# A hybrid attention and Mamba-2 block on one core: B of groups 1 to 7 is turned into rows through DRAM instead of on TensorE

## The chip, the core and the metric

The kernel runs on one core of a Trainium2 chip. Five engines work side by side, each through its own stream of instructions in a fixed order: TensorE (PE in the profile: matrix products and transposes), VectorE (DVE), ScalarE (ACT), GpSimd (POOL) and SyncE (SP). They wait for each other with semaphores. Transfers run on DMA queues, which SyncE and GpSimd fill here. The metric is the time of one execution on the device in microseconds (us); lower is better.

## What is computed

One layer of a decoder block: 512 tokens, 1024 channels, fp32. Two token mixers take the same normed input: an attention branch (12 heads, three dilated patterns) and an SSM branch (Mamba-2, 8 groups, 4 heads of 64 channels a group, 128 states). Their sum by learned gates goes through an output projection, and then through an MLP of 4096 hidden channels. The change touches the SSM branch alone. From the reference:

```python
xbc = jax.nn.silu(causal_conv(xbc) + conv_b)
xs, bm, cm = jnp.split(xbc, [SSM_INNER, SSM_INNER + SSM_GROUPS * SSM_STATE], axis=-1)
...
# ssd_chunked: 4 chunks c of 128 tokens (l, s), group g, head h of the group, state n, channel p
cb = jnp.einsum('bclgn,bcsgn->bcgls', cc, bc)
y_diag = jnp.einsum('bcghls,bcsghp->bclghp', cb[:, :, :, None] * decay, xd)
states = jnp.einsum('bclgn,bcghl,bclghp->bcghpn', bc, decay_states, xd)
_, prev = lax.scan(step, init, (states, chunk_decay))      # over the chunks
y_off = jnp.einsum('bclgn,bcghpn,bcghl->bclghp', cc, prev, jnp.exp(a_cs))
...
y = (y_diag + y_off + d_skip * xs) * silu(z)
y = rmsnorm_per_group(y, norm_w) @ w_ssm_proj
```

B (bc here) is used twice: in cb with the states as the summed axis, and in the states with the tokens as the summed axis. A product on TensorE sums over the partitions, so B is needed both ways: states on the partitions (as conv leaves it) and tokens on the partitions ("rows").

## The kernel before

**Precision.** A large fp32 product is made as three products of rounded halves: `split` makes the high half on ScalarE (line 96) and the low half as the rest on VectorE (line 99), and `three` issues high x high, high x low, low x high. Names ending in h and l are such halves (xsh, bkl, yth, ytl, wh_x). The scan's products of pcb, pyd, pyo and pn are made in full fp32.

**The weights.** A unit is a block of 256 weight columns, or rows for the projection: x (the SSM input), bc (B and C), z, sp (the SSM projection), gs and ga (gates). `prep` loads a unit through SyncE and splits it into one of two slots of wh and wl. A unit is 48 matmuls of 512 columns. A unit of x, bc or z makes two outputs of 24 matmuls each; sp makes eight outputs of 6. The splits of x's weights are put off (`held`) to the end of the third step of `ssm_group`.

**The order on TensorE.** Every matmul and transpose stays in program order (`mm`, `tr`: lines 227 and 230), and the program is interleaved by hand. `ssm_group(g)` is a generator with a `yield` between the steps of one group's scan; the units stand in a queue, `Filler`. The loop over the groups calls `fill.run(us)` ahead of each step, which issues matmuls of the queue worth that many us at 0.64 us for three of them, and the budgets of the seven steps come from a table, `SSM_FILL`, or `SSM_LAST` for group 7. So the unit matmuls cover the time that the other engines need between two steps. The queue's order is x0, bc0, then for each group x, bc, z, and sp of the group before.

**The steps of a group**, with the names that the profile shows:

1. xd (rows of x times dt), xs (times the decay to the chunk's end), split into xsh and xsl.
2. Three transposes pb turn B's first three chunks into rows, and `split` makes bkh (ScalarE) and bkl (VectorE) of them. Four products pcb of C and B; VectorE masks them into cbm (L812), and multiplies the decays w by cbm in four products (L816).
3. Nine matmuls pst of 256 columns make the states from bkh, bkl, xsh and xsl; the third is the first that reads bkl. VectorE chains them into prev (L826 to L830).
4. Sixteen products pyd of xd and w, six products pyo of prev and C; VectorE makes y of them (L845 to L856), through the scratch tile t1.
5. pn sums the squares of y; VectorE, GpSimd (rt, L215) and two transfers on GpSimd's queue (rt_d L873, rg L875) make the norm's factor as a row for every partition. Then `decays(g+1)` reads the next group's w on that queue (L774).
6. Nothing.
7. y is scaled (L882) and split into yth and ytl (ScalarE L96, VectorE L99), which sp of this group reads later.

VectorE adds each output of sp into acc (L729, `acc_evac`), and in group 0 ScalarE copies it instead. The scheduler places these adds early by a priority; it orders the other engines' instructions by priorities and by when their data come, except where `pin` keeps the program's order.

**x through DRAM.** x also needs rows. `to_rows` transposes 32 by 32 blocks on VectorE (L741), writes them to a scratch tensor in DRAM with four transfers of 64 KB on GpSimd's queue (L744), and `x_unit` reads it back as rows, xd, with one transfer of 512 KB (L757) on the same queue. B doesn't go this way before.

Of the kernel before, what the change touches and what calls it, by code (L numbers as in the profile page):

```python
# [11 lines left out]
F32 = mybir.dt.float32  # L12
# [6 lines left out]
P = 128  # L19
T = 512  # L20
NT = 4
# [5 lines left out]
GROUPS = 8  # L27
# [15 lines left out]
BIG = 1e30  # L43

FILL0, FILL1, FILLA, FILLB, FILLC = 3.0, 4.0, 3.0, 2.8, 2.8
SSM_FILL = (6, 4, 4, 3, 9.5, 5, 4.5)
SSM_LAST = (5, 6, 4, 3, 9, 8, 8)

V_ORDER = tuple((d, i) for d in (1, 0, 2) for i in range(NT))
V_STEPS = {(1, 0, 2): (("s", 2),), (1, 0, 5): (("t", 1),), (1, 0, 6): (("n", 2),), (1, 1, 1): (("s", 3),),  # L50
# [33 lines left out]
def hybrid_block(ctx: ExitStack, tc: tile.TileContext, a: dict):  # L84
    nc = tc.nc
    act, dve, pool, pe, sp = nc.scalar, nc.vector, nc.gpsimd, nc.tensor, nc.sync
# [5 lines left out]
    dram = ctx.enter_context(tc.tile_pool(name="dram", bufs=1, space=DRAM))  # L92


    def split(src, hi, lo, eng=None, pinned=False, lo_pinned=False):
        ins = act.activation(hi, src, AF.Copy)  # L96
        if pinned:
            tc.keep_in_program_order(ins)
        ins = (eng or dve).tensor_tensor(lo, src, hi.bitcast(F32), op=ALU.subtract)  # L99
        if lo_pinned:  # L100
            tc.keep_in_program_order(ins)
# [22 lines left out]
    held = []  # L124
# [37 lines left out]
    def v3(t, k):  # L162
        return t.rearrange("p (k n) -> p k n", k=k)
# [59 lines left out]
    def pin(ins):  # L223
        return tc.keep_in_program_order(ins)
# [4 lines left out]
    def tr(dst, src):  # L229
        tc.keep_in_program_order(pe.transpose(dst, src, ident))  # L230
# [27 lines left out]
    def abank(name):  # L258
        return psa.tile([P, T], F32, name=name, tag="a")
# [256 lines left out]
    def in_unit(key, evac):  # L516

        hi, lo = take(key)
        for c in range(2):
            ps = gbank(f"ps{key}_{c}")  # L520
            yield from gemm_part(ps, v3(hi, KD), v3(lo, KD), c, range(KD), KD, uhk, ulk)
            with tc.high_priority(offset=400):
                evac(c, ps)
        done()
# [103 lines left out]
    for key in ATT_UNITS:  # L628
        n, j = key[:-1], int(key[-1])
# [54 lines left out]
    sg = sctx.enter_context(tc.tile_pool(name="ssm", bufs=1, side="right", reuse_waits="tile"))  # L684
# [4 lines left out]
    def conv_silu(ct, ps, tag, bufs):  # L689
        h = sg.tile([P, T], F32, name=f"ch{ct}", tag="ch", bufs=2)  # L690
        act.activation(h, ps, AF.Identity, bias=cb_[:, ct : ct + 1], scale=cw[:, ct, 3:4])
        for d in (1, 2, 3):
            dve.scalar_tensor_tensor(h[:, d:], ps[:, : T - d], cw[:, ct, 3 - d : 4 - d], h[:, d:],
                                     op0=ALU.mult, op1=ALU.add)
        t = sg.tile([P, T], F32, name=f"ct{ct}", tag=tag, bufs=bufs)
        act.activation(t, h, AF.Tanh)
        dve.scalar_tensor_tensor(t, t, 1.0, h, op0=ALU.add, op1=ALU.mult)
        return t
# [32 lines left out]
        return evac  # L731

    convs = {}
    xrows, xds = {}, {}

    def to_rows(src, rows_, c0, tag, name):


        n = src.shape[-1]
        t = sg.tile([P, n], F32, name=f"sqt{name}", tag=tag, bufs=2)  # L740
        dve.transpose(t, src)  # L741
        for r in range(4):
            rs_ = slice(32 * r, 32 * r + 32)
            ins = pool.dma_start(rows_[:, c0 + 32 * r : c0 + 32 * r + 32].rearrange("(m i) j -> i m j", i=32),  # L744
                                 t[rs_, :].rearrange("i (m j) -> i m j", j=32))
            if c0:
                pin(ins)

    def x_unit(g):
        def evac(c, ps):  # L750
            convs[g, c] = conv_silu(2 * g + c, ps, "cx", 4)
            if c == 0:
                xrows[g] = dram.tile([T, UC], F32, name=f"x_d{g}")
            to_rows(convs[g, c], xrows[g], c * P, "sq", f"{g}_{c}")
            if c == 1:
                xds[g] = sg.tile([P, NT * UC], F32, name=f"xd{g}", tag="xd")
                pin(pool.dma_start(v3(xds[g], NT), xrows[g].rearrange("(k p) j -> p k j", p=P)))  # L757

        return in_unit(f"x{g}", evac)

    def bc_unit(g):
        def evac(c, ps):
            convs[g, 2 + c] = conv_silu(16 + 8 * c + g, ps, "cb" if c == 0 else "cc", 2)

        return in_unit(f"bc{g}", evac)

    TC = T - P
# [20 lines left out]
    def ssm_group(g, sz):  # L788
# [7 lines left out]
        dve.tensor_tensor(h64(xs), h64(xd[:, : 3 * UC]), bc64(ds_, g, 0, 3), op=ALU.mult)  # L796
        xsp = [sg.tile([P, 3 * UC], F32R, name=f"xs{n}{g}", tag=f"xs{n}") for n in "hl"]
        split(xs, *xsp)
        yield

        bt, ct = convs.pop((g, 2)), convs.pop((g, 3))
        bk = [sg.tile([P, TC], F32R, name=f"bk{n}{g}", tag=f"bk{n}") for n in "hl"]
        pb = abank(f"pb{g}")
        for c in range(3):
            tr(pb[:, c * P : (c + 1) * P], bt[:, c * P : (c + 1) * P])
        split(pb[:, :TC], *bk)
        pcb = abank(f"pcb{g}")
        for c in range(NT):
            cs = slice(c * P, (c + 1) * P)
# [4 lines left out]
        for c in range(NT):  # L814
            wv = w[:, c * HG : (c + 1) * HG, :]
            dve.tensor_tensor(wv, wv, cbm[:, c, :].unsqueeze(1).broadcast_to([P, HG, P]), op=ALU.mult)  # L816
        yield

        prev = sg.tile([P, 3, UC], F32, name=f"prev{g}", tag="prev")
        pst = [abank(f"pst{g}_{b}") for b in range(2)]  # L820
        for c in range(3):
            pv = pst[c // 2][:, (c % 2) * UC : (c % 2 + 1) * UC]
            bs, us = slice(c * P, (c + 1) * P), slice(c * UC, (c + 1) * UC)
# [19 lines left out]
        for j in range(2):  # L843
# [6 lines left out]
            t1 = sg.tile([P, TC], F32, name=f"t1{g}_{j}", tag="t1", bufs=2)  # L850
# [46 lines left out]
    for g in range(GROUPS):  # L897
        fill.add(f"x{g}", x_unit(g))
        fill.add(f"bc{g}", bc_unit(g))
        if g == 0:  # L900
            for j in (2, 3):
                fill.add(f"ap{j}", att_unit(j))
        else:
            fill.add(f"z{g}", z_unit(g, szs[g]))
            fill.add(f"sp{g-1}", project_unit(g - 1, acc_evac(g - 1)))
# [4 lines left out]
    for g in range(GROUPS):  # L910
        steps = ssm_group(g, szs[g])
        fill.through(f"bc{g}")
        for n, us in enumerate(SSM_LAST if g == GROUPS - 1 else SSM_FILL):
            fill.run(us)
            if n == 3 and g > 0:
                fill.through(f"z{g}")
            next(steps, None)
# [293 lines left out]
    us = {}  # L1211
# [67 lines left out]
    j = last  # L1279
# [106 lines left out]
```

## Time and profile before

| | |
|---|---|
| time, median of 3 runs (lowest to highest) | 1086.37 us (1086.25 to 1086.47) |
| the profiled execution: its own time | 1084.77 us |
| its span, from the first to the last instruction | 1083.0 us |
| mean granted clock of TensorE | 0.999 |
| TensorE busy | 1068.3 us, 99% of the span |
| VectorE busy | 741.4 us, 68% |
| ScalarE busy | 532.9 us, 49% |
| GpSimd busy | 120.1 us, 11% |

In the stage that holds the scan's groups 0 to 7 (250 to 655 us of the span), the windows view gives 400.1 us of TensorE in 405, 342.1 of VectorE and 212.1 of ScalarE. The time of an execution is longer than its span by what lies around the first and the last instruction (1.8 us here). A row of the timeline has the start and the length of an instruction in us, the engine, its line, the operation with its output and its inputs, the shapes, and how many instructions it stands for; a bracket at its end says how long the engine was idle ahead of it, and for whom.

### The profile page before, as it was taken

What the parts mean: (1) busy time and instruction counts of PE and PEld (TensorE: products, weight loads), DVE (VectorE), ACT (ScalarE), POOL (GpSimd) and SP (SyncE); (2) the same over time, 40 slices, a digit from 0 to 9 for tenths busy, and PEclk for the clock granted to TensorE, in tenths of its full rate; (3) what the DMA queues carried; (4) which work ended last, traced back from release to release, by engine and by line L of the source; (5) the groups of instructions that cost most, each with busy time, mean ns of one, the idle gap of its engine ahead of it and who ended that gap; (6) DMA issues with size and microseconds to landing.
All of it is one profiled execution on the core that took longest, in us unless ns stands there. A gap on an engine that the chain in (4) does not pass through costs nothing.

```text
span 1083.0 us, 14771 instructions
## 1 busy us (share of the span) xinstructions
PE 1068.3 (99%) x5895; PEld 908.5 (84%) x5895; DVE 741.4 (68%) x1104; ACT 532.9 (49%) x921; POOL 120.1 (11%) x159
## 2 busy tenths in 40 slices
PE   9999999999999999999999999999999999999997
PEld 8988787778778878888888878889899998888886
DVE  6657666436877889897979795868687785342324
ACT  6356656526375645546273723454466665332222
POOL 2203122002031211202030300010000000000000
PEclk9999999999999999999999999999999999999999
DMA  8232122224453544434454423540233324233202
GB/s 278 86 102 75 61 78 68 93 83 111 152 126 118 127 132 111 141 103 146 132 143 144 127 91 114 204 146 2 78 121 113 118 81 144 107 124 110 82 35 78
DMA packets 90853, 121.44 MB, mean 112 GB/s; under 512 B 5776, under 2 KB 75920, under 8 KB 89760
## 3 DMA queue, kind: packets, MB, share of 16 engines
q1 hardware_dynamic: 85216, 101.01, 29.1%
q0 software_dynamic: 5424, 19.49, 6.7%
q8 instruction: 46, 0.75, 0.3%
q14 instruction: 23, 0.19, 0.1%
q10 hardware_dynamic: 144, 0.00, 0.0%
HBM read 114.11 MB, written 6.37 MB: 111 GB/s over the span
## 4 chain that ended last, share of the span: by engine, by line
PE 89%; DVE 6%; ACT 1%; issue 1%; DMA 1%; POOL 0%; POOLq 0%; DVEq 0%; ACTq 0%
PE psd L227 16%; PE psx L227 8%; PE psbc L227 8%; PE psz L227 8%; PE psuX L227 6%; PE pssp L227 5%; PE psu L227 4%; PE psga L227 4%; PE psgs L227 4%; PE psv L227 3%; PE psk L227 3%; PE psq L227 3%; PE psuZ L227 3%; PE psap L227 3%; PE psuY L227 1%; PE pq L227 1%
## 5 line engine op out<-in xcount | busy, mean ns | idle before, releaser
L227 PE MATMUL psd<-wh_dn,hh 128*128 128x512 f32 x240 | 93.4, 389 | 0.0
L227 PE MATMUL psd<-wl_dn,hh 128*128 128x512 f32 x240 | 93.4, 389 | 0.0
L227 PE MATMUL psd<-wh_dn,hl 128*128 128x512 f32 x240 | 93.4, 389 | 0.0
L99 DVE TENSOR_TENSOR hl<-hidden,hh 128x512 fp32r<-128x512 f32 x31 | 21.1, 692 | 71.4 <-ACT hh L96 71.3
L96 ACT ACTIVATE hh<-hidden 128x512 fp32r<-128x512 f32 x31 | 19.1, 628 | 92.0 <-PE psd L227 92.0
L227 PEld LDWEIGHTS psd<-wh_dn,hl 128*128 128x128 f32 x240 | 45.0, 188 | 9.4
L227 PEld LDWEIGHTS psd<-wh_dn,hh 128*128 128x128 f32 x240 | 45.0, 188 | 9.4
L227 PEld LDWEIGHTS psd<-wl_dn,hh 128*128 128x128 f32 x240 | 45.0, 188 | 9.2
L227 PE MATMUL psx<-uh,wl_x 128*128 128x512 f32 x128 | 50.0, 390 | 1.8 <-DVE wl_x L99 1.8
L227 PE MATMUL pssp<-yth,wh_sp 128*128 128x512 f32 x128 | 51.1, 400 | 0.0
L227 PE MATMUL psx<-uh,wh_x 128*128 128x512 f32 x128 | 50.6, 396 | 0.0
L227 PE MATMUL pssp<-ytl,wh_sp 128*128 128x512 f32 x128 | 50.2, 392 | 0.3 <-DVE ytl L99 0.3
L227 PE MATMUL pssp<-yth,wl_sp 128*128 128x512 f32 x128 | 50.1, 392 | 0.0
L227 PE MATMUL psz<-uh,wh_z 128*128 128x512 f32 x128 | 50.0, 391 | 0.0
L227 PE MATMUL psbc<-uh,wh_bc 128*128 128x512 f32 x128 | 49.9, 390 | 0.0
L227 PE MATMUL psz<-uh,wl_z 128*128 128x512 f32 x128 | 49.9, 390 | 0.0
L227 PE MATMUL psx<-ul,wh_x 128*128 128x512 f32 x128 | 49.8, 389 | 0.0
L227 PE MATMUL psz<-ul,wh_z 128*128 128x512 f32 x128 | 49.8, 389 | 0.0
L227 PE MATMUL psbc<-uh,wl_bc 128*128 128x512 f32 x128 | 49.8, 389 | 0.0
L227 PE MATMUL psbc<-ul,wh_bc 128*128 128x512 f32 x128 | 49.8, 389 | 0.0
L744 POOL DMA_DIRECT2D x_d<-sqt x64 | 41.6, 657 | 72.8 <-DVE sqt L741 72.3
L96 ACT ACTIVATE wh_bc<-ws_bc 128x1024 fp32r<-128x1024 f32 x16 | 16.7, 1055 | 60.6 <-PE pssp L227 53.3
(362 smaller groups left out, 3291.6 us busy)
## 6 DMA issues: line engine op xcount, KB each, us to landing
ws_up<-in_w_up_dram SPq DMA_DIRECT2D x16, 1024.0 KB, 5.6
ws_dn<-in_w_down_dram SPq DMA_DIRECT2D x15, 1024.0 KB, 5.0
ws_z<-in_w_in_dram SPq DMA_DIRECT2D x8, 1024.0 KB, 7.5
ws_x<-in_w_in_dram SPq DMA_DIRECT2D x8, 1024.0 KB, 6.3
w<-acs_d POOLq DMA_DIRECT2D x8, 1024.0 KB, 5.8
ws_bc<-in_w_in_dram SPq DMA_DIRECT2D x16, 512.0 KB, 5.2
ws_sp<-in_w_ssm_proj_dram SPq DMA_DIRECT2D x8, 1024.0 KB, 4.9
ws_ga<-in_w_in_dram SPq DMA_DIRECT2D x4, 1024.0 KB, 6.0
```

What stands on the lines that cost most here:

```text
L96: ins = act.activation(hi, src, AF.Copy)
L99: ins = (eng or dve).tensor_tensor(lo, src, hi.bitcast(F32), op=ALU.subtract)
L227: tc.keep_in_program_order(pe.matmul(*args, **kw))
L744: ins = pool.dma_start(rows_[:, c0 + 32 * r : c0 + 32 * r + 32].rearrange("(m i) j -> i m j", i=32), t[rs_, :].rearrange("i (m j) -> i m j ...
```

## The change

Three things change together. First, the rows of B in groups 1 to 7 no longer come from transposes on TensorE. When conv has made B, its first three chunks go through `to_rows` as x does: a 32 by 32 transpose on VectorE (128 x 384, into a buffer of t1), four writes to b_d on GpSimd's queue, and a read back into br (192 KB, tag t1) on that queue, all pinned to the program's order. Group 0 keeps the transposes. Second, the split into bkh and bkl stands behind the second `yield`, ahead of pst, in those groups. Third, the table of budgets: group 0 gets one of its own, and the budgets ahead of the second and third steps grow while the fifth shrinks, so that more of sp lies ahead of pcb and pst and less ahead of pn. `while held and g == 0` in the first step finds nothing to do in the order that is built. All lines behind the tables move down by one, and by up to eleven in `ssm_group`.

```diff
-SSM_FILL = (6, 4, 4, 3, 9.5, 5, 4.5)
-SSM_LAST = (5, 6, 4, 3, 9, 8, 8)
+SSM_FIRST = (6, 4, 4, 4, 8.5, 5, 4.5)
+SSM_FILL = (6, 6, 4.5, 3.5, 7, 5, 4.5)
+SSM_LAST = (6, 7, 5, 4, 8, 8, 8)
...
     def to_rows(src, rows_, c0, tag, name):
...
-            if c0:
+            if c0 or tag == "t1":
                 pin(ins)
...
     def bc_unit(g):
         def evac(c, ps):
             convs[g, 2 + c] = conv_silu(16 + 8 * c + g, ps, "cb" if c == 0 else "cc", 2)
+            if c == 0 and g > 0:
+                rows_ = dram.tile([TC, P], F32, name=f"b_d{g}")
+                to_rows(convs[g, 2][:, :TC], rows_, 0, "t1", f"b{g}")
+                brs[g] = sg.tile([P, TC], F32, name=f"br{g}", tag="t1", bufs=2)
+                pin(pool.dma_start(v3(brs[g], NT - 1), rows_.rearrange("(k p) j -> p k j", p=P)))
...
         split(xs, *xsp)
+        while held and g == 0:
+            held.pop()()
         yield
...
-        pb = abank(f"pb{g}")
-        for c in range(3):
-            tr(pb[:, c * P : (c + 1) * P], bt[:, c * P : (c + 1) * P])
-        split(pb[:, :TC], *bk)
+        if g == 0:
+            pb = abank(f"pb{g}")
+            for c in range(3):
+                tr(pb[:, c * P : (c + 1) * P], bt[:, c * P : (c + 1) * P])
+            split(pb[:, :TC], *bk)
         pcb = abank(f"pcb{g}")
...
         yield
+        if g > 0:
+            split(brs.pop(g), *bk)
...
-        for n, us in enumerate(SSM_LAST if g == GROUPS - 1 else SSM_FILL):
+        for n, us in enumerate(SSM_FIRST if g == 0 else SSM_LAST if g == GROUPS - 1 else SSM_FILL):
```

On TensorE, groups 2 to 6 have, before: 48 matmuls of z, the 3 of pb, pcb, 18 of sp, the 9 of pst, 15 of sp, pyd and pyo, 15 of sp, 30 of x, pn, 18 of x, 48 of bc. Now: 48 of z, 9 of sp, pcb, 21 of sp, the 9 of pst, 18 of sp, pyd and pyo, 33 of x, pn, 15 of x, 48 of bc. Group 1 goes from z to sp, 12, to pcb, and then has 21 of sp ahead of pst; group 7 has 15 ahead of pcb and 24 between pcb and pst.

The order on VectorE changes at the middle of each group. In group 3 before, from cbm to the first of the four products of w (acc0 and so on are the adds of sp's outputs, pssp2 those of group 2):

```order
L812 TENSOR_TENSOR cbm3_3751<-pcb3_3746,tri_198 128x512
L543 SCALAR_TENSOR_TENSOR sz3_1_3757<-sz3_1_3757,psz3_1_3706 128x512
L99 TENSOR_TENSOR xsl3_3717<-xs3_3714,xsh3_3716 128x768
L729 TENSOR_TENSOR acc0_2897<-acc0_2897,pssp2_0_3762 128x512
L729 TENSOR_TENSOR acc1_2906<-acc1_2906,pssp2_1_3770 128x512
L99 TENSOR_TENSOR bkl3_3739<-pb3_3740,bkh3_3738 128x384
L816 TENSOR_TENSOR w3_3530<-w3_3530,cbm3_3751 128x512
L729 TENSOR_TENSOR acc2_2915<-acc2_2915,pssp2_2_3778 128x512
```

And now, in the same group:

```order
L730 TENSOR_TENSOR acc0_2887<-acc0_2887,pssp2_0_3762 128x512
L100 TENSOR_TENSOR xsl3_3736<-xs3_3733,xsh3_3735 128x768
L821 TENSOR_TENSOR cbm3_3781<-pcb3_3776,tri_198 128x512
L730 TENSOR_TENSOR acc1_2909<-acc1_2909,pssp2_1_3770 128x512
L825 TENSOR_TENSOR w3_3543<-w3_3543,cbm3_3781 128x512
L730 TENSOR_TENSOR acc2_2918<-acc2_2918,pssp2_2_3791 128x512
L825 TENSOR_TENSOR w3_3543<-w3_3543,cbm3_3781 128x512
L730 TENSOR_TENSOR acc3_2927<-acc3_2927,pssp2_3_3799 128x512
L825 TENSOR_TENSOR w3_3543<-w3_3543,cbm3_3781 128x512
L730 TENSOR_TENSOR acc4_2936<-acc4_2936,pssp2_4_3807 128x512
L825 TENSOR_TENSOR w3_3543<-w3_3543,cbm3_3781 128x512
L100 TENSOR_TENSOR bkl3_3775<-br3_3646,bkh3_3774 128x384
```

bkl stood ahead of w's four products and behind acc1; now it stands behind all four and behind acc4.

In group 1 the order on ScalarE changes where y of group 0 is split. Before, around z of group 1 (ch25 and ct25 belong to the conv of C, wh_x2 is the weight of x of group 2, in two halves):

```order
L542 ACTIVATE sz1_0_2831<-psz1_0_2798 128x512
L696 ACTIVATE ct25_2787<-ch25_2782 128x512
L96 ACTIVATE yth0_2802<-y0_0_2582 128x512
L96 ACTIVATE wh_x2_2938<-ws_x2_2869 128x1024
L542 ACTIVATE sz1_1_2866<-psz1_1_2834 128x512
L96 ACTIVATE yth0_2802<-y0_1_2594 128x512
L96 ACTIVATE xsh1_2847<-xs1_2845 128x768
L96 ACTIVATE bkh1_2875<-pb1_2877 128x384
```

And now:

```order
L543 ACTIVATE sz1_0_2840<-psz1_0_2807 128x512
L697 ACTIVATE ct25_2796<-ch25_2791 128x512
L97 ACTIVATE wh_x2_2961<-ws_x2_2878 128x1024
L543 ACTIVATE sz1_1_2875<-psz1_1_2843 128x512
L97 ACTIVATE xsh1_2856<-xs1_2854 128x768
L97 ACTIVATE wh_x2_2961<-ws_x2_2878 128x1024
L97 ACTIVATE yth0_2811<-y0_0_2588 128x512
L97 ACTIVATE bkh1_2896<-br1_2764 128x384
L97 ACTIVATE yth0_2811<-y0_1_2600 128x512
```

The first half of yth stood ahead of wh_x2, and now stands behind both halves of it and behind xsh. On GpSimd's queue, B's four writes stand behind the writes of x's second half; in group 1 two of them come ahead of the read of xd, two behind it, and then rg and the read of br. Before, rg stood ahead of the read of xd.

More of the change, by code (lines that the diff above doesn't have):

```diff
@@ L733, in hybrid_block @@
     convs = {}
-    xrows, xds = {}, {}
+    xrows, xds, brs = {}, {}, {}
     def to_rows(src, rows_, c0, tag, name):
```

## The prediction

> **What bounds the kernel now.** I read the page first, then the waits of TensorE, then the timelines of TensorE, VectorE and ScalarE in the stage of the scan (255 to 655 us of the span), the only stage that the change touches.
>
> ```profile
> span 1083.0 us, 14771 instructions
> ...
> PE 1068.3 (99%) x5895; PEld 908.5 (84%) x5895; DVE 741.4 (68%) x1104; ACT 532.9 (49%) x921; POOL 120.1 (11%) x159
> ...
> PEclk9999999999999999999999999999999999999999
> ...
> PE 89%; DVE 6%; ACT 1%; issue 1%; DMA 1%; POOL 0%; POOLq 0%; DVEq 0%; ACTq 0%
> ```
>
> TensorE is busy 99% of the span at full clock, and 89% of the chain that ended last is its own work. So two things move the time: matmuls that go away, and waits of TensorE that come or go. Work on the other engines costs only where it becomes such a wait. The waits that stand in this stage:
>
> ```profile
> PE pyd L227 <- DVE w L816: 2.7, 7, 0.6
> ...
> PE pssp L227 <- DVE ytl L99: 0.3, 1, 0.3
> ```
>
> The second number is how often. Group 3 of the scan, on TensorE; the first column is the start, the second the length, and since matmuls overlap, the cost of one is the distance to the next start:
>
> ```profile
> 423.32 0.49 PE L230 MATMUL pb<-ident,ct 128*128 128x128 f32 x3
> 423.64 1.06 PE L227 MATMUL pcb<-ct,ct 128*128 128x128 f32 x8
> 424.46 0.47 PE L227 MATMUL pssp<-yth,wh_sp 128*128 128x512 f32 x1
> ...
> 428.44 0.39 PE L227 MATMUL pssp<-yth,wl_sp 128*128 128x512 f32 x1
> 428.66 0.28 PE L227 MATMUL pst<-xsh,bkh 128*128 128x256 f32 x1
> ...
> 428.90 0.28 PE L227 MATMUL pst<-xsh,bkl 128*128 128x256 f32 x1
> ...
> 432.95 0.39 PE L227 MATMUL pssp<-yth,wl_sp 128*128 128x512 f32 x1
> 433.27 0.88 PE L227 MATMUL pyd<-w,xd 128*64 128x128 f32 x12
> 434.53 1.31 PE L227 MATMUL pyd<-w,xd 128*64 128x128 f32 x20 [0.39 <-DVE w L816]
> 435.77 1.60 PE L227 MATMUL pyo<-ct,prev 128*128 128x128 f32 x12
> ...
> 437.68 0.39 PE L227 MATMUL pssp<-yth,wl_sp 128*128 128x512 f32 x1
> ```
>
> And VectorE in the same group:
>
> ```profile
> 428.11 0.55 DVE L99 TENSOR_TENSOR bkl<-pb,bkh 128x384 fp32r<-128x384 f32 x1
> 428.58 0.68 DVE L816 TENSOR_TENSOR w<-w,cbm 128x512 f32<-128x512 f32 x1
> 429.18 0.68 DVE L729 TENSOR_TENSOR acc<-acc,pssp 128x512 f32<-128x512 f32 x1
> ...
> 438.11 0.69 DVE L729 TENSOR_TENSOR acc<-acc,pssp 128x512 f32<-128x512 f32 x1 [0.24 <-PE pssp L227]
> ```
>
> Two things are to be seen. The low half of B, bkl, is ready at 428.11 + 0.55 = 428.66, and the third matmul of pst, the first that reads it, starts at 428.90: 0.24 us of slack. And an acc add that waits for its matmuls starts 438.11 - 437.68 = 0.43 us after the start of the last of them.
>
> **Part 1: the transposes go.** The three transposes of pb take 423.64 - 423.32 = 0.32 us. The products of pcb then follow a 512-wide matmul directly, and such a step into full-precision products costs 433.27 - 432.95 = 0.32 instead of the usual 0.22 (428.44 to 428.66), so about 0.1 of it stays. That is 0.23 net in each of groups 1 to 7; group 0 keeps its transposes. Six groups make -1.4 us (-1.9 if nothing stays); group 1 is counted whole in part 4.
>
> **Part 2: the wait of pyd for w.** From pyd to pyo group 3 takes 435.77 - 433.27 = 2.50 us with its wait; group 1, which does not wait, shows what it takes without; group 7 waits twice. TensorE in groups 1 and 7:
>
> ```profile
> 333.38 1.97 PE L227 MATMUL pyd<-w,xd 128*64 128x128 f32 x32
> 335.27 1.60 PE L227 MATMUL pyo<-ct,prev 128*128 128x128 f32 x12
> ```
>
> ```profile
> 632.42 0.28 PE L227 MATMUL pst<-xsl,bkh 128*128 128x256 f32 x1
> 632.80 0.39 PE L227 MATMUL pst<-xsh,bkl 128*128 128x256 f32 x1
> ...
> 637.22 0.66 PE L227 MATMUL pyd<-w,xd 128*64 128x128 f32 x8
> ...
> 640.34 1.60 PE L227 MATMUL pyo<-ct,prev 128*128 128x128 f32 x12
> ```
>
> Without a wait it is 335.27 - 333.38 = 1.89. So groups 2 to 6 lose 0.61 each and group 7 loses 640.34 - 637.22 - 1.89 = 1.23. In the new order all four w products stand ahead of bkl on VectorE, and pst, which needs bkl, stands ahead of pyd on TensorE: pyd can no longer wait for w. All of it goes: 5 x 0.61 + 1.23 = -4.3 us.
>
> **Part 3: what is late next is bkl.** The split of B moved behind the second yield. On VectorE of groups 2 to 6 it now stands behind cbm, the adds acc1 to acc4 and all four w products, where it stood behind acc0 and acc1. On TensorE 21 matmuls of sp lie between pcb and pst, and with the 9 ahead of pcb they are 30: six for each output, so acc4 waits for the very matmul ahead of pst. Call the start of pst T. That last matmul starts 0.22 before T, so acc4 starts at T + 0.21; an add or a w product takes VectorE 0.60 (428.58 to 429.18); so w's last product starts at T + 0.81, bkl at T + 1.41, and bkl is ready at T + 1.96. The third matmul of pst would start at T + 0.24. TensorE waits 1.72 us, in five groups: +8.6. This holds however early VectorE is, since acc4 ties it to TensorE; if VectorE is late it is more.
>
> In group 7, 15 and 24 matmuls of sp lie ahead of pst, so acc5 (36 of the 39) starts at T - 0.47, then come three w products and bkl: 0.60 + 3 x 0.60 + 0.55 gives T + 2.48, a wait of 2.24. Its present wait at that place, 632.80 - 632.42 less the usual 0.12 = 0.26, goes. Net +2.0. Part 3 is +10.6; my bounds for a wait are 1.2 (if adds and products overlap more) and 2.4 (VectorE 0.7 behind).
>
> **Part 4: group 1, y of group 0.** Here acc is made by ScalarE, so part 3's tie is missing, but another one forms. ScalarE, then VectorE, then TensorE around the start of sp0:
>
> ```profile
> 319.49 0.63 ACT L96 ACTIVATE yth<-y 128x512 fp32r<-128x512 f32 x1 [1.73 <-DVE y L882]
> 321.86 1.06 ACT L96 ACTIVATE wh_x<-ws_x 128x1024 fp32r<-128x1024 f32 x1 [1.73 <-PE psz L227]
> 322.83 0.58 ACT L542 ACTIVATE sz<-psz 128x512 f32<-128x512 f32 x1
> ...
> 323.82 0.83 ACT L96 ACTIVATE xsh<-xs 128x768 fp32r<-128x768 f32 x1
> ...
> 324.92 1.06 ACT L96 ACTIVATE wh_x<-ws_x 128x1024 fp32r<-128x1024 f32 x1
> ```
>
> ```profile
> 323.43 0.69 DVE L543 SCALAR_TENSOR_TENSOR sz<-sz,psz 128x512 f32<-128x512 f32 x1 [0.71 <-ACT sz L542]
> 324.04 0.69 DVE L99 TENSOR_TENSOR ytl<-y,yth 128x512 fp32r<-128x512 f32 x1
> ```
>
> ```profile
> 321.88 0.39 PE L227 MATMUL pssp<-yth,wh_sp 128*128 128x512 f32 x1
> ...
> 324.78 0.50 PE L227 MATMUL pssp<-ytl,wh_sp 128*128 128x512 f32 x1 [0.31 <-DVE ytl L99]
> ```
>
> Now the first yth is made at 319.49, ahead of wh_x, which waits for the last matmul of z1. In the new order of ScalarE it stands behind wh_x, sz, xsh and the second wh_x. From 321.86 these take, by the distances and lengths above, about 0.97 + 0.5 + 0.75 + 0.95, so yth starts near 325.0 and is there at 325.6: the first matmul of sp0 comes at 325.65, not 321.88, a wait of 3.8 us. Then ytl (0.69) lets the second go at 326.35. Behind it VectorE scales the second y, makes bkl, and makes the second ytl after ScalarE's second yth: about 0.65, 0.55 and 0.65 + 0.7, so the fifth matmul starts near 328.4 instead of 324.78, and pcb (0.82 + 0.1) still follows where it was done before. Net 328.4 - 324.8 + 0.9 = +4.5 us; 2.5 if xsh and the second wh_x slip behind yth's data less than I think, 6 if the DMA queue is late.
>
> That queue is GpSimd's: B's writes stand behind x's and, in group 1, ahead of the read of xd and of rg.
>
> ```profile
> x_d<-sqt POOLq DMA_DIRECT2D x64, 64.0 KB, 2.5
> xd<-x_d POOLq DMA_DIRECT2D x8, 512.0 KB, 4.4
> ...
> rg<-rt_d POOLq DMA_DIRECT2D x8, 256.0 KB, 3.6
> ```
>
> The last column is us to landing. A B of its own (48 KB writes, one 192 KB read) should take 2.5 and 3.6 to 4.4 after four issues: some 10 us after its transpose. From conv of B to pst lie the rest of bc, all of z (48 matmuls, 10.9 us) and 30 matmuls of sp (6.8 us), so the read is hidden in groups 2 to 7 by some 7 us. The added 32-by-32 transpose and the five issues lie beside TensorE's matmuls: 0. The moved pn (33 matmuls of x after pyo) I cost at nothing: VectorE needs about 7.5 us from pyd's first y to it, and 33 x 0.22 us of x and pyo's 1.36 lie between.
>
> **The sum.** -1.4 - 4.3 + 10.6 + 4.5 = +9.4 us. The profiled execution, 1084.77 us, becomes 1094.2; the median of the three runs lies 1.6 above that execution, so 1095.8.
>
> **Rivals.** First, *the gains alone*: bkl and yth are in time, and only parts 1 and 2 count, -1.6 with group 1's share and -4.3: 1080.5, faster. It needs the third matmul of pst at least 1.7 us later against acc4 than I place it, eight matmuls of sp; for it speaks only that the new fill numbers move pst later after pcb by three matmuls, against it that acc4's own matmul is the one ahead of pst. Chance 0.11. Second, *they cancel*: waits of 0.8 us instead of 1.72 and 2 us in group 1, about 1087: 0.04. Third, *B's read is late*: with small pieces of 128 bytes the queue runs 8 us later than in its rows, bkh waits in every group, and each us beyond the cover costs 7: with 1 us, 1103. The rows of x_d, in the same pieces, speak against it. 0.06.
>
> Fourth, *the clock drops in group 1*. In the rows the clock stays full through the longest wait there is. At the very start, before any load, it reads otherwise:
>
> ```profile
> 1.16 5.33 PE L227 MATMUL warm<-ones 128*128 128x128 f32 x28 [1.16 <-POOL ones L218]
> ```
>
> That is 0.19 us a record against 0.10 in pcb (0.82 for 8), half speed. If a wait of 3.8 us brings that back for as long again, up to 5.3 us of work takes double, half of it under the waits that follow anyway: +1 to +2.6, about 1097.6. Chance 0.14. [...]
>
> My own forecast keeps 0.65.
>
> **The numbers.** Runs of this kernel agree within 0.02% (1086.25 to 1086.47), so 0.2% (2.2 us) can be told. Part 3 between its bounds (1.2 and 2.4 for six waits) gives -3.1 to +4.1, part 4 -2 to +1.5, part 1 -0.5. The low end, 1089, is both lows together and a little more; the high, 1102, both highs with the clock. Faster 0.11, same 0.05, slower 0.84.
>
> **What would show it.** Right: a new wait of TensorE for bkl of about 1.7 us in groups 2 to 7, no wait of pyd for w, and sp0's first matmuls waiting near 4 us for yth, then ytl. Wrong: pst without a wait, or the largest new wait ending on a DMA of br; a granted clock below full after sp0's start shows the fourth rival.

## The result and the profile after

The changed kernel takes 1100.14 us (1098.81 to 1102.11, 4 runs), the kernel before 1086.31 us beside it. The ratio is 1.0134 (95% interval 1.0121 to 1.0147), so the change costs 13.8 us. The profiled execution took 1098.81 us with a span of 1097.0, 14.0 more than the profiled one before. The page, with the busy times of the engines, and below it the waits of TensorE:

```profile
span 1097.0 us, 14792 instructions
...
PE 1070.7 (98%) x5874; PEld 909.5 (83%) x5874; DVE 746.7 (68%) x1111; ACT 536.6 (49%) x921; POOL 143.7 (13%) x194
```

```profile
PE pst L228 <- DVE bkl L100: 10.2, 6, 2.1
PE pssp L228 <- ACT yth L97: 4.6, 2, 4.3
```

The wait of pyd for w is gone from the list, and two new waits stand at its head, those of the forecast. Here is the middle of group 3 on TensorE and on VectorE:

```profile
438.79 0.39 PE L228 MATMUL pssp<-yth,wl_sp 128*128 128x512 f32 x1
439.01 0.28 PE L228 MATMUL pst<-xsh,bkh 128*128 128x256 f32 x1
...
441.03 0.39 PE L228 MATMUL pst<-xsh,bkl 128*128 128x256 f32 x1 [1.62 <-DVE bkl L100]
```

```profile
439.21 0.69 DVE L730 TENSOR_TENSOR acc<-acc,pssp 128x512 f32<-128x512 f32 x1
439.82 0.68 DVE L825 TENSOR_TENSOR w<-w,cbm 128x512 f32<-128x512 f32 x1
440.42 0.55 DVE L100 TENSOR_TENSOR bkl<-br,bkh 128x384 fp32r<-128x384 f32 x1
```

With T = 439.01, the start of pst, acc4 starts at T + 0.20, the last product of w at T + 0.81 and bkl at T + 1.41; the prediction had 0.21, 0.81 and 1.41. The third matmul of pst starts at T + 2.02 instead of T + 0.24. That is 1.78 us in each of the groups 2 to 6, and 2.30 in group 7 (2.42 from the second matmul of pst to the third there, less 0.12).

Group 1 on TensorE, ScalarE, VectorE and GpSimd's queue:

```profile
321.62 0.39 PE L228 MATMUL psz<-uh,wl_z 128*128 128x512 f32 x1
326.26 0.79 PE L228 MATMUL pssp<-yth,wh_sp 128*128 128x512 f32 x1 [4.26 <-ACT yth L97]
...
328.69 0.79 PE L228 MATMUL pssp<-yth,wh_sp 128*128 128x512 f32 x1 [0.39 <-ACT yth L97]
329.41 0.79 PE L228 MATMUL pssp<-ytl,wh_sp 128*128 128x512 f32 x1
```

```profile
323.99 1.04 ACT L97 ACTIVATE wh_x<-ws_x 128x1024 fp32r<-128x1024 f32 x1
325.58 0.63 ACT L97 ACTIVATE yth<-y 128x512 fp32r<-128x512 f32 x1 [0.55 <-DVE y L893]
```

```profile
324.79 0.75 DVE L893 SCALAR_TENSOR_TENSOR y<-y,nw,rg 128x512 f32<-128x512 f32 x1 [0.72 <-DMA rg<-rt_d]
```

```profile
314.63 1.22 POOL L745 DMA_DIRECT2D b_d<-sqtb  x2 [3.33 <-DVE sqtb L742]
315.84 0.79 POOL L758 DMA_DIRECT2D xd<-x_d  x1
316.62 1.24 POOL L745 DMA_DIRECT2D b_d<-sqtb  x2
317.85 0.57 POOL L886 DMA_DIRECT2D rg<-rt_d  x1
```

sp0 waits 4.41 us (326.26 - 321.62 - 0.23). ScalarE makes yth behind both halves of the weight, as forecast, but it also stood idle for 0.55 us ahead of yth: y came later still, because rg, issued at 317.85 behind B's writes and xd, landed only when VectorE could start y, at 324.79. Two chains end within 0.55 us of each other, and rg's is the later one.

The last new thing is the clock. In the windows of 1 us, the third number behind the stretch is the granted clock (behind the busy time and its count):

```profile
326.00:327.00 1.00, 0.74 (x1) 0.50 0.23 67
...
332.00:333.00 1.00, 1.00 (x4) 0.59 0.06 16
...
650.00:651.00 1.00, 1.00 (x7) 0.63 0.00 0
651.00:652.00 1.00, 1.00 (x4) 0.50 0.00 0
652.00:653.00 1.00, 1.00 (x4) 0.50 0.00 0
653.00:654.00 1.00, 1.00 (x5) 0.66 0.00 0
```

At the end of the wait of group 1, and also behind the wait of 2.30 us of group 7, TensorE runs at half speed; behind the five waits of 1.78 us it does not.

### The profile page after: what moved, and what is told of

It is laid out like the page before. It is cut to its first block, busy times and chain, and to the rows that moved or that the text cites. A ratio compares the mean times of both kernels' runs of the same rounds, so it can differ in the third digit from the quotient of the medians.

```text
span 1097.0 us, 14792 instructions
## 1 busy us (share of the span) xinstructions
PE 1070.7 (98%) x5874; PEld 909.5 (83%) x5874; DVE 746.7 (68%) x1111; ACT 536.6 (49%) x921; POOL 143.7 (13%) x194
## 4 chain that ended last, share of the span: by engine, by line
PE 84%; DVE 7%; ACT 4%; DMA 3%; issue 1%; POOL 0%; SPq 0%; POOLq 0%; DVEq 0%; ACTq 0%
PE psd L228 15%; PE psx L228 8%; PE psbc L228 6%; PE psuX L228 6%; PE psz L228 6%; PE pssp L228 6%; PE psu L228 4%; PE psga L228 4%; PE psgs L228 4%; PE psk L228 3%; PE psq L228 3%; PE psuZ L228 3%; PE psap L228 3%; PE psv L228 3%; PE psuY L228 1%
## 5 line engine op out<-in xcount | busy, mean ns | idle before, releaser
L694 DVE SCALAR_TENSOR_TENSOR ch<-psx,cw,ch 128x511 f32<-128x511 f32 (+2 forms) x48 | 35.6, 742 | 14.6 <-ACT ch L692 13.1
```

## The experiments

The theory was the prediction's: two places in an order cost the time, bkl's on VectorE and yth's with rg's on its queue. Its rivals were that B's way through DRAM is late as such, and that the new budgets cost. All eleven kernels ran beside the kernel before; each ratio is to it.

**1. bkl earlier** (short name bkl_early).

```diff
-            dve.tensor_tensor(wv, wv, cbm[:, c, :]...)
+            ins = dve.tensor_tensor(wv, wv, cbm[:, c, :]...)
+            if c == 0 and g > 0:
+                with tc.issue_after(ins.ins):
+                    split(brs.pop(g), *bk)
...
-        if g > 0:
-            split(brs.pop(g), *bk)
```

> The changed kernel, but on VectorE the low half of B stands right behind the first of the four products of w in groups 1 to 7 instead of behind the fourth (in group 7 behind the first and two adds). Theory (the place of bkl in VectorE's order makes the waits of pst): the five waits of 1.78 us and the one of 2.30 us go, and the half clock behind the last one too (about 1.65 us), and pyd doesn't wait for w; 1100.1 - 12.8 = about 1087.3 us. Rival (B's read through DRAM is what comes late, bkl would wait for it wherever it stands): waits of the same size stay, now at bkh or bkl for br, 1097 to 1102 us. Second rival (the gain comes back as waits of pyd for w, as in the kernel before): 1091 us.

Measured: 1097.25 us, ratio 1.0108 (1.0095 to 1.0121). Pst no longer waits, pyd does not wait either, and yet only 2.9 of the 12.8 us came back. The waits of TensorE now:

```profile
PE pssp L228 <- ACT yth L97: 8.7, 5, 3.6
...
PE pssp L228 <- DVE ytl L100: 1.5, 3, 0.9
```

Neither rival foresaw this: in groups 3, 5 and 7 sp stops ahead of its fourth matmul. The trace of experiment 3 shows it without group 1's disturbance.

**2. rg ahead of B's writes in group 1** (rg_ahead).

```diff
-                to_rows(convs[g, 2][:, :TC], rows_, 0, "t1", f"b{g}")
+                with tc.issue_after(rgs[g - 1].ins) if g == 1 else ExitStack():
+                    to_rows(convs[g, 2][:, :TC], rows_, 0, "t1", f"b{g}")
```

> The changed kernel, but in group 1 the read of rg stands ahead of B's writes on GpSimd's queue, as it stood ahead of the read of xd before; with it the first half of yth stands ahead of the weight's high half on ScalarE again. Theory (rg's place in the queue makes y of group 0 late, and the order on ScalarE follows from that): sp0's first matmul waits less than 0.5 us, the half clock behind it goes, group 1 gives back 7.1 us: about 1093.0 us, and the waits of pst for bkl stay as they are. Rival (the added transfers of B make the queue late in any order): rg still lands near 324 us, sp0 waits 3 us or more, over 1097 us.

Measured: 1095.63 us, ratio 1.0088 (1.0074 to 1.0102), 4.5 us less than the change instead of 7.1. GpSimd's queue and TensorE there:

```profile
310.93 0.58 POOL L887 DMA_DIRECT2D rg<-rt_d  x1
314.27 0.63 POOL L745 DMA_DIRECT2D b_d<-sqtb  x1 [2.76 <-DVE sqtb L742]
```

```profile
321.49 0.39 PE L228 MATMUL pssp<-yth,wh_sp 128*128 128x512 f32 x1
...
323.57 0.50 PE L228 MATMUL pssp<-yth,wh_sp 128*128 128x512 f32 x1 [1.25 <-ACT yth L97]
324.38 0.50 PE L228 MATMUL pssp<-ytl,wh_sp 128*128 128x512 f32 x1 [0.30 <-DVE ytl L100]
```

sp0's first matmul no longer waits. With rg early the first half of yth also stands ahead of the weight on ScalarE again, so this one move cures both chains. The fourth, the first that reads the second half of yth, waits now (2.0 us with ytl behind it), and 3.4 us of half clock follow.

**3. Both moves** (both_moved): the edits of 1 and 2.

> The two moves of the first two kernels together: bkl behind the first product of w, and rg ahead of B's writes in group 1. Theory: the losses add up and both go, what is left is the change's gain, 4.3 us of pyd's waits and 1.6 of transposes: 1100.1 - 12.8 - 7.1 = 1080.2 us, 6 us faster than before. Rival (with TensorE earlier, another wait takes their place, B's read in group 1 or pyd's wait for w): 1083 to 1087 us.

Measured: 1093.24 us, ratio 1.0073 (1.0058 to 1.0089). The gains of 1 and 2 add up (2.9 + 4.5 = 7.4, 6.9 measured), but neither is whole. ScalarE in group 5:

```profile
526.10 1.06 ACT L97 ACTIVATE wh_x<-ws_x 128x1024 fp32r<-128x1024 f32 x1 [2.31 <-PE psz L228]
527.06 0.58 ACT L543 ACTIVATE sz<-psz 128x512 f32<-128x512 f32 x1
527.54 0.62 ACT L97 ACTIVATE yth<-y 128x512 fp32r<-128x512 f32 x1
```

The second half of yth stands behind the weight's high half, whose slot is only free with z's last matmul, and behind sz. sp begins right behind z, so it runs into this. In the kernel before pb and pcb, 1.1 us together, stood between z and sp in groups 2 to 6. This is a third loss, which the waits for bkl and rg had covered.

**4. Matmuls without work in two of the waits** (clock_kept). The kernel computes the same, with 27 matmuls more that nothing reads.

```diff
+        if g == 0:
+            keep_clock(18)      # ahead of sp0's first matmul
...
+        if g == GROUPS - 1:
+            keep_clock(9)       # ahead of pst of group 7
```

> The changed kernel with matmuls that do no work of the reference's (their result is not read) in two of TensorE's waits: 18 of 512 columns ahead of sp0's first in group 1, 9 ahead of pst in group 7. Both fit inside the waits (4.1 and 2.0 us of 4.4 and 2.3). Theory (TensorE's granted clock falls to half because TensorE stood still, and costs 1.6 us in group 1 and 1.65 in group 7 beside the waits themselves): the clock stays at 1.00 behind both, about 1096.9 us, and the runs spread less than the 3.3 us of the changed kernel. Rival (the matmuls were slow there for another reason, such as the transfers of that moment): the half rate stays, 1100 us or more.

Measured: 1098.21 us, ratio 1.0111 (1.0097 to 1.0126), against 1.0134 (1.0121 to 1.0147): the intervals overlap, the median lies between the two expectations, and the runs spread no less (1095.43 to 1099.36), so the time alone settles little. The windows show it for group 7; the first stretch here holds the nine matmuls:

```profile
649.00:651.00 2.00, 2.00 (x11) 1.00 0.00 0
651.00:653.00 2.00, 1.90 (x13) 1.00 0.00 0
331.00:332.00 1.00, 1.00 (x4) 0.72 0.06 16
...
334.00:335.00 1.00, 1.00 (x6) 0.57 0.00 0
```

The same pst and sp run at full clock there once TensorE has not stood still. In group 1 a later wait (1.10 us for the second yth) was left, and half of the half-clock stretch with it.

The profiled execution has one more stretch of half clock, which has nothing to do with this edit. It follows a wait for the low half of x's weight that every kernel here has at this place:

```profile
285.86 0.50 PE L228 MATMUL psx<-uh,wl_x 128*128 128x512 f32 x1 [1.78 <-DVE wl_x L100]
```

```profile
287.00:288.00 1.00, 1.00 (x4) 0.54 0.00 0
```

The same stretch stands in the profiles of experiments 6 and 9, and in none of the other ten. So half clock can come or stay away behind one and the same wait (1.78 us); the last section lists the cases.

**5. yth first** (yth_first): both moves, and in step 7

```diff
-            pin(dve.scalar_tensor_tensor(ys[j], ys[j], nw[...], rstd, ...))
-            split(ys[j], yt[0][:, j, :], yt[1][:, j, :])
+            with tc.high_priority(offset=400):
+                dve.scalar_tensor_tensor(ys[j], ys[j], nw[...], rstd, ...)
+                split(ys[j], yt[0][:, j, :], yt[1][:, j, :])
```

> The kernel with both moves (bkl behind the first product of w, rg ahead of B's writes in group 1), and y's scaling and split at a higher priority in every group: on ScalarE both halves of yth now stand ahead of the weight's high half, where in groups 1, 3, 5 and 7 the second half stood behind it. Theory (a third loss took the place of the first two: sp starts 9 matmuls ahead of pcb, and the second half of yth waits on ScalarE behind a weight's half that waits for the last matmul of z): the waits of sp for yth and ytl (2.0 us in groups 1, 3 and 5, 3.8 in group 7) and the half clock behind them go, 1078.5 to 1082 us, faster than before by 4 to 8. Rival (y of the group before is itself late by the new budgets, whatever the order on ScalarE): waits of more than 1 us stay in those groups, 1087 to 1093 us.

Measured: 1082.08 us, ratio 0.9967 (0.9954 to 0.9980): faster than before, 11.2 us less than experiment 3, at the upper edge of what was expected. No wait of sp is left. What stands at the head of TensorE's waits now is a fourth one:

```profile
PE pn L228 <- DVE sq L872: 2.3, 4, 0.6
```

The profiled execution (1083.92 us) also has a wait of 1.97 us for ft behind the scan, with half clock from 722.56 on. The edit touches nothing there; experiment 2's profile has the same wait (1.98 us), all others 0.5 us or less, and no run here says why. It is a reason to compare medians, and stretches of the scan, rather than whole spans of single profiles.

**6. pcb ahead of sp again** (pcb_first): both moves, bkl behind the second product of w, and

```diff
-SSM_FILL = (6, 6, 4.5, 3.5, 7, 5, 4.5)
-SSM_LAST = (6, 7, 5, 4, 8, 8, 8)
+SSM_FILL = (6, 4, 6.5, 3.5, 7, 5, 4.5)
+SSM_LAST = (5, 6, 7, 4, 8, 8, 8)
```

> The kernel with both moves (bkl behind the second product of w here), and two numbers of the budgets set back so that pcb stands ahead of sp again in groups 2 to 6 as before (30 matmuls of sp between pcb and pst; group 7 has 6 and 33, group 1 has 3 and 30). Theory (sp's start ahead of pcb is what leaves yth too little time): the waits of sp for yth shrink by pcb's 0.9 to 1.1 us, below 0.9 us in each group, with no half clock or little: 1080 to 1085 us. Rival (the waits come from the added transfers and stay): 1090 us or more.

Measured: 1082.40 us, ratio 0.9973 (0.9962 to 0.9984). Sp's waits are gone in groups 2 to 7 and shrink to 1.2 us in group 1; in group 7 pst waits 1.70 us for bkl. Either cure of the third loss works, so it is the meeting of sp's earlier start with yth's place that costs.

**7. The budgets alone** (budgets_alone): the kernel before with the three new tables.

> The kernel before with the new budgets alone: B's transposes on TensorE, no transfers of B. bkl stands ahead of cbm in groups 2 to 6, yth ahead of the weight except in group 1. Theory: the waits of pyd for w go (4.3 us), nothing comes in groups 2 to 6, and group 1 takes a wait of sp for the second half of yth as with rg ahead (2.0 us and some half clock): 1083 to 1086 us, faster than before by 0 to 3. Rival (the new budgets are what costs, also without B's transfers): slower than before, 1089 us or more.

Measured: 1084.30 us, ratio 0.9987 (0.9978 to 0.9996). The new numbers are no loss; they take pyd's waits away.

**8. B through DRAM alone** (dram_alone): the changed kernel with the old tables.

> The changed kernel with the budgets of before: B through DRAM, split behind the second yield, 18 matmuls of sp between pcb and pst. bkl stands behind the second product of w. Theory: group 1 loses as in the changed kernel (rg behind B's writes: 5.5 us and half clock), pst waits for bkl 0.3 to 1 us in groups 2 to 6, the transposes are saved (1.4), and pyd's wait for w stays in part: 1090 to 1096 us. Rival (B's path costs nothing, the budgets made the loss): 1084 to 1087 us.

Measured: 1109.61 us, ratio 1.0226 (1.0213 to 1.0240), far over both expectations. Group 3 on TensorE and VectorE:

```profile
438.39 0.28 PE L228 MATMUL pst<-xsl,bkh 128*128 128x256 f32 x1
441.49 0.42 PE L228 MATMUL pst<-xsh,bkl 128*128 128x256 f32 x1 [2.82 <-DVE bkl L100]
```

```profile
439.08 1.89 DVE L825 TENSOR_TENSOR w<-w,cbm 128x512 f32<-128x512 f32 x3
440.88 0.55 DVE L100 TENSOR_TENSOR bkl<-br,bkh 128x384 fp32r<-128x384 f32 x1
```

I had misread the order: bkl stands behind all four products of w there too, and with 18 matmuls instead of 30 from pcb to pst VectorE is further behind. The wait is 2.98 us, and behind each of the five such waits 3.4 us of half clock follow. The new budgets thus belong to the change: without them each wait for bkl is two thirds longer, and half clock follows it. In group 1 sp0's first matmul waits here as in the changed kernel (4.20 us for yth), and in experiment 7 it does not: that wait comes with B's transfers, under either budgets.

**9. bkl late, B by transposes** (bkl_late_alone): the kernel of 7 with bkl behind the fourth product of w.

```diff
-        split(pb[:, :TC], *bk)
+        act.activation(bk[0], pb[:, :TC], AF.Copy)
...
         yield
+        if g > 0:
+            with tc.issue_after(ins.ins):      # ins: the fourth product of w
+                dve.tensor_tensor(bk[1], pb[:, :TC], bk[0].bitcast(F32), op=ALU.subtract)
```

> The kernel before with the new budgets and B's transposes on TensorE, no transfers of B, and one edit: bkl in groups 1 to 7 behind the fourth product of w on VectorE, as the change puts it. Theory (VectorE's order alone makes the waits of pst, B's way through DRAM has no part in them): pst waits for bkl 1.78 us in groups 2 to 6 and 2.30 in group 7, half clock behind the last; the kernel with the budgets alone, 1084.3, plus 11.2 and 1.7 = 1097 us. Rival (the waits came from the late arrival of B's rows): pst waits less than 0.5 us, 1085 to 1087 us.

Measured: 1093.28 us, ratio 1.0070 (1.0058 to 1.0083), 9.0 us over experiment 7.

```profile
PE pst L228 <- DVE bkl L823: 8.0, 6, 1.5
```

By starts the six waits are 5 x 1.45 + 1.70 = 8.95 us, as much as the medians differ by. The profiled executions differ by 12.1: the one of this run has two stretches of half clock, behind waits that both kernels have (from 285.36 and from 326.32), and the one of experiment 7 has none. The six waits are shorter than forecast because the fourth product of w stands ahead of acc4 here, and behind none of these six does the clock fall. The rival falls: without any transfer of B, its place on VectorE makes the wait.

**10. pn later** (pn_later): experiment 5 with two budgets changed.

```diff
-SSM_FILL = (6, 6, 4.5, 3.5, 7, 5, 4.5)
+SSM_FILL = (6, 6, 4.5, 3.5, 7.3, 4.7, 4.5)
```

> The kernel with yth first, and 36 instead of 33 matmuls of x ahead of pn in groups 2 to 6 (two budgets by 0.3 us). There pn waited 0.73 us for the sum of squares in groups 3 to 6. Theory: these waits go, 1082.1 - 2.9 = 1079.2 us. Rival (three matmuls less behind pn make rg, and with it yth, late): waits of sp for yth return, 1082 us or more.

Measured: 1079.72 us, ratio 0.9942 (0.9929 to 0.9954). The waits of pn are gone, and a wait of 1.10 us for bkl in group 7 is left.

**11. yth first, no transfers of B** (no_dram_yth_first): experiment 7 with the edit of 5.

> The kernel before with the new budgets and with y's scaling and split at the higher priority, B's transposes on TensorE and no transfers of B. Theory: group 1's wait of sp goes (2.0 us and half clock in some runs), 1081 to 1082.5 us, so that B's way through DRAM is worth at most the transposes, 1.6 us, beside the same budgets and order. Rival (the budgets only work with the transposes gone): no better than the budgets alone, 1084 us or more.

Measured: 1079.78 us, ratio 0.9946 (0.9933 to 0.9960), better than both expectations. What B's way through DRAM is worth stands in the distance from pcb to pcb, one whole group, here from group 3 to 4 in the kernels of 10 and of 11:

```profile
423.33 1.05 PE L228 MATMUL pcb<-ct,ct 128*128 128x128 f32 x8
472.97 1.05 PE L228 MATMUL pcb<-ct,ct 128*128 128x128 f32 x8
```

```profile
424.70 1.06 PE L228 MATMUL pcb<-ct,ct 128*128 128x128 f32 x8
474.70 1.06 PE L228 MATMUL pcb<-ct,ct 128*128 128x128 f32 x8
```

49.64 against 50.00 us (49.63 and 49.99 in the mean over groups 2 to 6). The three transposes cost 0.36 us a group, 2.5 us in seven groups, and group 7 gives 1.10 back, so about 1.4 us should be left. The lowest runs are that far apart (1078.07 and 1079.49); the medians are not (0.06 us). In the five executions of 10 the granted clock was 0.997 to 0.999, in those of 11 always 0.999, so half clock in some executions of 10 can have hidden the gain; that is not shown. By the medians, then, the best two kernels are equal, one with the transfers and one without; what they share is the budgets and the order.

## Why the prediction held, and where it did not

The time, 1100.14 us, lies inside the range (1089 to 1102), 4.3 above the number, on the side that was forecast. Step by step:

- **The place of bkl**, the largest term: right in its mechanism and nearly in size. 1.78 for 1.72 us and 2.30 for 2.24. Experiment 9 shows that the order alone does it.
- **pyd's wait for w**: right in size, but the reason given isn't needed. The prediction let it go because w's products stand ahead of bkl; in experiments 1 and 7 bkl stands ahead of at least three of them, and pyd doesn't wait either. The budgets alone do it (experiment 7), and with the old budgets the late bkl does it too (experiment 8). The group's length shows the size, pcb to pcb: 474.20 - 423.64 = 50.56 us before, 474.20 from this row and 423.64 from the prediction's, and 49.99 with the new budgets and the transposes; 0.57 where I said 0.61.

```profile
474.20 1.06 PE L227 MATMUL pcb<-ct,ct 128*128 128x128 f32 x8
```

- **The transposes**: 0.36 us a group instead of the 0.23 I took; the 0.1 that I let stay for pcb behind a 512-wide matmul did not stay.
- **Group 1**: the wait was foreseen, its cause only in part. I read ScalarE's order and put yth at 325.0; it came at 325.58, for rg, whose place in the queue I had named as a risk and not as the cause. That two chains end within 0.55 us of each other is why the size came out near; that part is luck. The fifth matmul of sp came at 329.41 instead of 324.78 in the kernel before, 4.63 later, and pcb's 0.92 follows it now: 5.55 for my 4.5. That ScalarE's order alone would have cost nearly as much is argued from the row, not tried, since the move of rg changed both.
- **The clock**: I had this as a rival with 0.14, for group 1 only. It came beside my own case, not instead of it, and in group 7 as well. From the rows, the last eight of the twelve matmuls of sp lose about 1.7 us in group 1 (3.51 instead of 1.81), and group 7 loses about 1.6 (six of sp at 0.42 instead of 0.23, pst from its third matmul on 1.35 instead of 0.93). This is the step of the sum that was missing: 3.3 of the 4.6 us by which the profiled difference, 14.0, exceeds my 9.4; group 1 has another 1.05. One reading under that rival does not hold: the slow matmuls at the very start were taken for half clock, but the windows view grants 1.00 there (1 to 6 us). So no row of before shows the 1 to 2.6 us of that rival, nor the share of the clock in the upper end of the range; the changed kernel shows 1.7 and 1.6 us in their place.
- **B's read is hidden**: right with less to spare. In group 3 ScalarE waited for it and made bkh from 435.48; with bkl right behind it, pst would have been in time until about 438.1, so 2.6 us were left and not 7. B's writes took 4.6 us to land (median), where 2.5 had been taken.

```profile
435.48 0.53 ACT L97 ACTIVATE bkh<-br 128x384 fp32r<-128x384 f32 x1 [0.99 <-DMA br<-b_d]
```

- **The range and the noise**: the upper end was added up short. Both highs and the clock's 1 to 2.6 us give 1102.4 to 1104, not 1102. And runs of the kernel before don't agree within 0.02%: the 39 that ran beside the experiments lie between 1084.15 and 1086.87 us.

The kernel's groups 2 to 6 add up: 50.56 - 0.57 - 0.36 + 1.78 = 51.41, and pcb to pcb after is 484.80 - 433.33 = 51.47.

```profile
433.33 1.05 PE L228 MATMUL pcb<-ct,ct 128*128 128x128 f32 x8
484.80 1.05 PE L228 MATMUL pcb<-ct,ct 128*128 128x128 f32 x8
```

What the prediction did not see is what lay under the two waits: taking them away gave back 6.9 of some 20 us, because sp's earlier start met yth's place on ScalarE. My rival *the gains alone*, 1080.5 us, is reached only when that third loss and pn's are cured as well (1079.72 us in experiment 10), or when B's transfers are left out (1079.78 in experiment 11).

## What to carry to other kernels

A step that is moved behind a `yield` is moved on every engine that it uses: here four w products came ahead of an instruction of 0.55 us that TensorE needed first, and the waits for it sum to 11.2 us (5 x 1.78 + 2.30). When a wait is taken away, look for the next one that it covered before the gain is counted; here yth lay under bkl and rg, and pn under yth. A wait on TensorE can cost more than its length: in these runs the matmuls behind some waits ran at half speed for 3.4 us or twice that. A single wait with 1.62 us or less in its bracket never did this here, one with 1.78 us did in three profiles of thirteen, and every one with 2.14 us or more did.

## What the runs showed of the hardware

Half clock came in stretches of one length. Added up over the windows of group 7, the missing clock is 0.37 + 0.50 + 0.50 + 0.34 = 1.71 us, that is 3.42 us at half speed; group 1 had twice that. In the experiments, between 240 and 800 us, the windows of 0.5 us miss 1.70 or 1.71 us in each stretch, or 3.42. In windows of 20 ns the two stretches of the changed kernel begin at 326.00 and 650.26:

```profile
326.00:326.02 0.02, 0.00 (x0) 0.53 0.66 205
650.26:650.28 0.02, 0.02 (x2) 0.70 0.00 0
```

The first begins 0.26 us ahead of the matmul that ends its wait (326.26), the second 0.40 us behind it (649.86).

How long TensorE has to stand still for this is no single number in these runs. Take its idle time as the brackets of the timeline give it, or as the windows of 0.5 us do:

- 2.14 us or more: half clock came behind every such wait, the 2.14 and 4.26 us of the changed kernel and the 4.20 and five times 2.82 us of experiment 8 among them.
- 1.97 us for ft in experiment 5: it came. 1.98 us for ft in experiment 2: it did not (1.00 in every window from 732 to 739 us).
- 1.78 us for x's weight: it came in experiments 4, 6 and 9, and in none of the other ten profiles.
- A single wait of 1.62 us or less: it never came. The five waits of the changed kernel (1.78 us by starts) are 1.62 us in their brackets.
- Two waits of sp with one matmul between, 1.54 or 1.55 us together (1.25 and 0.30): in experiments 1 and 3 it came in group 5 and not in group 3; in group 1 it came in experiments 2, 3 and 9, and not in experiment 7. In experiment 4 it came in group 1 behind 1.10 and 0.23 us.

What decides between the cases of 1.3 to 2 us is not shown, nor why two short waits can do what a single wait of 1.62 us does not.

A stretch of half clock may also be the 1.6 us between the kernel before's profiled execution and its median. Of the 39 executions on record, the 15 of 1084.89 us or less had a granted clock of 0.998 or 0.999, and the 24 of 1085.78 us or more had 0.997; one stretch, 1.7 us of clock missing, is 0.16% of the time. The kernel before has the wait for x's weight, too (1.8 us). But no execution of the longer kind was profiled, so the place is not shown.
